# Rotary embedding: adding on VectorE alone, with one GpSimd product per tile

## The chip, the cores and the metric

The kernel runs on one core of a Trainium2 chip. The metric is device time in microseconds, the median of several executions. TensorE, VectorE (DVE in the profile), ScalarE (ACT), GpSimd (POOL) and SyncE (SP) run at the same time, each through its own queue of instructions, and wait for one another by semaphores. Transfers between the chip's memory (HBM) and the core's on-chip memory (SBUF, 128 partitions) are issued by SP and ACT and run on 16 DMA engines. PSUM is a second, small on-chip memory, which TensorE writes and which VectorE and ScalarE can read and write.

## What is computed

`x` has shape (8, 2048, 8, 64): batch, position, head, element. Each head's 64 elements are two halves of 32, which are rotated by an angle of their position:

```
x1, x2 = x[..., :32], x[..., 32:]
out1 = x1 * cos - x2 * sin
out2 = x1 * sin + x2 * cos
```

`cos` and `sin` have shape (2048, 32) and serve all batches and heads. All is float32. The input is 33.5 MB and the output as much.

## The kernel before

Each partition holds 16 consecutive positions ("rows") of one batch. A row is 8 heads of 64 elements, so 512 elements or 2 KB, and a batch is a tile `xt` of 128 partitions by 8192 elements, 32 KB in each partition and 4 MB in all. Five such buffers exist (`NBUF`). Batches 0 to 4 are loaded at the beginning from SP's queue, batch 0 in three parts (lines 64 to 71); batches 5 to 7 are loaded when the stores of batches 0 to 2 have left their buffers. Stores are issued from ACT's queue (line 74). All of these instructions are kept in program order on their queues.

A batch is worked in pieces of 4 rows (2048 elements); the first batch begins, and the last ends, with two pieces of 2 rows. `rotate` (line 101) knows three kinds of piece:

- Kind A, all pieces but the five named below: GpSimd makes `t2`, the other half times sine, in two instructions, one with `sin_sb` for the second halves and one with the negated table `nsin` for the first (line 121). VectorE makes `t1 = x * cos` in PSUM (line 128) and adds both back into `xt` (line 135).
- Kind B, the first piece of batches 2, 4 and 5: the products are the same, but TensorE adds them, by two matmuls with a unit matrix into PSUM (lines 140 and 141), and ScalarE copies the sum into `xt` (line 142).
- Kind C, the first piece of batches 1 and 3: VectorE makes both products (lines 128 and 145) and GpSimd none; TensorE adds or subtracts them with `eye` or `neye` (lines 156 and 157), and ScalarE copies (line 161).

`cos_ps` and `sin_ps` are copies of the tables in PSUM. The product `t2` has three buffers, so GpSimd can be ahead of VectorE by that many pieces; `t1` of kind A has one. The store of a whole batch is issued once its pieces are added; batch 0 is stored in parts of 1, 1, 2, 4 and 8 rows, each issued when the add that it depends on is done, and the last batch in parts of 8, 4 and 4 rows.

Of the kernel before, what the change touches and what calls it, by code (L numbers as in the profile page):

```python
# [9 lines left out]
@with_exitstack  # L10
def kernel(
    ctx: ExitStack,
    tc: tile.TileContext,
    x: bass.AP,
    cos: bass.AP,
    sin: bass.AP,
    out: bass.AP,
):
    nc = tc.nc
    keep = tc.keep_in_program_order  # L20
    f32 = mybir.dt.float32
    PSUM = bass.MemoryType.PSUM

    B, S, H, D = x.shape
    Dh = D // 2
    P = 128
    HD = H * D
    R = S // P
    ROW = R * HD
    UNIT = 4 * HD  # L30
    NBUF = 5
    C = 512
    last = B - 1

    xv = x.rearrange("b (q r) h d -> b q (r h d)", q=P)
    ov = out.rearrange("b (q r) h d -> b q (r h d)", q=P)
    cos_src = cos.rearrange("(q r) d -> q r d", q=P)
    sin_src = sin.rearrange("(q r) d -> q r d", q=P)

    const_pool = ctx.enter_context(tc.tile_pool(name="const", bufs=1))  # L40
    tab_pool = ctx.enter_context(tc.tile_pool(name="tab", bufs=1, space=PSUM))
    t1_pool = ctx.enter_context(tc.tile_pool(name="t1p", bufs=1, space=PSUM))
    o_pool = ctx.enter_context(tc.tile_pool(name="op", bufs=2, space=PSUM))
    t1s_pool = ctx.enter_context(tc.tile_pool(name="t1s", bufs=2))
    xpool = ctx.enter_context(tc.tile_pool(name="xpool", bufs=NBUF))
    t2_pool = ctx.enter_context(tc.tile_pool(name="t2p", bufs=3))

    cos_sb = const_pool.tile([P, R, Dh], f32, tag="cb")
    sin_sb = const_pool.tile([P, R, Dh], f32, tag="sb")
    nsin = const_pool.tile([P, R, Dh], f32, tag="ns")  # L50
    eye = const_pool.tile([P, P], f32, tag="eye")
    neye = const_pool.tile([P, P], f32, tag="neye")
    cos_ps = tab_pool.tile([P, R, Dh], f32, tag="cp")
    sin_ps = tab_pool.tile([P, R, Dh], f32, tag="sp")

    xts = {}

    def spans(sizes):
        lo = 0
        for n in sizes:  # L60
            yield lo, n
            lo += n

    def load(b):
        xt = xpool.tile([P, ROW], f32, tag="xt", name=f"xt{b}")
        for lo, n in spans([UNIT, UNIT, 2 * UNIT] if b == 0 else [ROW]):
            keep(nc.sync.dma_start(out=xt[:, lo : lo + n], in_=xv[b, :, lo : lo + n]))  # L67
            if b == 0 and lo == 0:
                keep(nc.sync.dma_start(out=cos_sb, in_=cos_src))  # L69
                keep(nc.sync.dma_start(out=sin_sb, in_=sin_src))  # L70
        xts[b] = xt

    def store(b, lo, n):
        keep(nc.scalar.dma_start(out=ov[b, :, lo : lo + n], in_=xts[b][:, lo : lo + n]))

    for b in range(NBUF):
        load(b)

    nc.gpsimd.memset(eye, 0.0)  # L79
    nc.gpsimd.affine_select(  # L80
        out=eye,
        in_=eye,
        compare_op=mybir.AluOpType.not_equal,
        fill=1.0,
        base=0,
        pattern=[[-1, P]],
        channel_multiplier=1,
    )
    keep(nc.scalar.mul(nsin, sin_sb, -1.0))  # L89
    keep(nc.scalar.copy(sin_ps, sin_sb))  # L90
    keep(nc.scalar.mul(neye, eye, -1.0))
    keep(nc.vector.tensor_copy(cos_ps, cos_sb))  # L92

    def rep(a, n):
        return dataclasses.replace(a, ap=[a.ap[0][:], a.ap[1][:], [0, n], a.ap[-1][:]])

    kinds = {}
    for b, kind in ((1, "C"), (2, "B"), (3, "C"), (4, "B"), (5, "B")):
        kinds[(b, 0)] = kind

    def rotate(b, lo, n):
        kind = kinds.get((b, lo), "A")
        xt = xts[b][:, lo : lo + n]
        r0 = lo // HD
        nr = n // HD
        xk = xt.rearrange("p (r k d) -> p r k d", r=nr, d=Dh)
        xu = xt.rearrange("p (g u d) -> p g u d", u=2, d=Dh)
        if kind == "A":
            t1 = t1_pool.tile([P, n], f32, tag="t1")
        else:  # L110
            t1 = t1s_pool.tile([P, n], f32, tag="t1s")
        if kind == "C":
            t2 = t1s_pool.tile([P, n], f32, tag="t1s")
        else:
            t2 = t2_pool.tile([P, n], f32, tag="t2")
        t1u = t1.rearrange("p (g u d) -> p g u d", u=2, d=Dh)
        t2u = t2.rearrange("p (g u d) -> p g u d", u=2, d=Dh)
        if kind != "C":
            for u, tab in ((1, sin_sb), (0, nsin)):
                keep(  # L120
                    nc.gpsimd.tensor_mul(  # L121
                        out=t2u[:, :, u, :].rearrange("p (r h) d -> p r h d", h=H),
                        in0=xu[:, :, 1 - u, :].rearrange("p (r h) d -> p r h d", h=H),
                        in1=rep(tab[:, r0 : r0 + nr, :], H),
                    )
                )
        keep(
            nc.vector.tensor_mul(  # L128
                out=t1.rearrange("p (r k d) -> p r k d", r=nr, d=Dh),
                in0=xk,  # L130
                in1=rep(cos_ps[:, r0 : r0 + nr, :], 2 * H),
            )
        )
        if kind == "A":
            keep(nc.vector.tensor_add(out=xt, in0=t1, in1=t2))  # L135
        elif kind == "B":
            for j in range(n // C):
                o = o_pool.tile([P, C], f32, tag="o")
                cs = slice(j * C, (j + 1) * C)
                nc.tensor.matmul(o, eye, t1[:, cs], start=True, stop=False)  # L140
                nc.tensor.matmul(o, eye, t2[:, cs], start=False, stop=True)  # L141
                keep(nc.scalar.copy(xt[:, cs], o))  # L142
        else:
            keep(
                nc.vector.tensor_mul(  # L145
                    out=t2.rearrange("p (r k d) -> p r k d", r=nr, d=Dh),
                    in0=xk,
                    in1=rep(sin_ps[:, r0 : r0 + nr, :], 2 * H),
                )
            )  # L150
            G = C // Dh
            for u in range(2):
                for j in range(n // 2 // C):
                    o = o_pool.tile([P, C], f32, tag="o")
                    gs = slice(j * G, (j + 1) * G)
                    nc.tensor.matmul(o, eye, t1u[:, gs, u, :], start=True, stop=False)  # L156
                    nc.tensor.matmul(  # L157
                        o, eye if u else neye, t2u[:, gs, 1 - u, :], start=False, stop=True
                    )
                    keep(  # L160
                        nc.scalar.copy(  # L161
                            xu[:, gs, u, :], o.rearrange("p (g d) -> p g d", d=Dh)
                        )
                    )

    def pieces(b):
        if b == 0:
            return [2 * HD, 2 * HD, UNIT, UNIT, UNIT]
        if b == last:
            return [UNIT, UNIT, UNIT, 2 * HD, 2 * HD]  # L170
        return [UNIT] * 4

    for b in range(B):
        done = 0
        outs = list(spans([2 * UNIT, UNIT, UNIT] if b == last else [ROW]))
        for lo, n in spans(pieces(b)):
            rotate(b, lo, n)
            done = lo + n
            while outs and sum(outs[0]) <= done:
                whole = outs.pop(0)  # L180
                if b == 0:
                    for part in spans([HD, HD, 2 * HD, UNIT, 2 * UNIT]):
                        store(b, *part)
                else:
                    store(b, *whole)
        if b + NBUF <= last:
            load(b + NBUF)

# [29 lines left out]
```

## Time and profile before

| | before |
|---|---|
| median of 10 executions | 163.63 us (163.4 to 164.75) |
| the profiled execution | 163.91 us, its span 162.1 us |
| VectorE busy | 140.1 us (86%) in 66 instructions |
| GpSimd busy | 138.9 us (86%) in 70 instructions |
| TensorE matmul busy | 47.2 us (29%) in 80 instructions |
| ScalarE busy | 14.3 us (9%) in 24 instructions |
| DMA | 67.65 MB, 417 GB/s over the span |

The span is the time between the first and the last event of the profiled execution; what lies between it and the execution's time is start and end outside the profile. Times in the profile's lines are microseconds from the span's start. Groups list the source line, the engine, the operation, what it writes and reads, the shape, the count, then total busy time, mean nanoseconds of one, and the idle time ahead of it with what ended that. Lines of DMA issues give the size and the median time from issue to landing.

### The profile page before, as it was taken

The numbers are of one execution on the slowest core, as the hardware profiler recorded it, in microseconds if no ns is written. First come the engines' busy times: TensorE is split into PE (matmuls) and PEld (weight loads), VectorE is DVE, ScalarE is ACT, GpSimd is POOL, SyncE is SP. The second block draws the span as 40 slices with busy tenths as digits, with TensorE's granted clock in tenths as the row PEclk, the third lists the DMA queues.
The fourth block names the chain that finished last, engine by engine and source line by source line (L and its number), as shares of the span: only waits on it lengthen the run. The fifth ranks groups of instructions, "written<-read, shape, count | busy, mean of one in ns | idle before, by whom it ended". The sixth has DMA issues, their size and how long they took to land.

```text
span 162.1 us, 470 instructions
## 1 busy us (share of the span) xinstructions
PE 47.2 (29%) x80; PEld 18.9 (12%) x80; DVE 140.1 (86%) x66; ACT 14.3 (9%) x24; POOL 138.9 (86%) x70
## 2 busy tenths in 40 slices
PE   0000000497009950892039903991000000000000
PEld 0000000142004410440023302340000000000000
DVE  0468999999999999999999999999999999999600
ACT  3300000013000220041001210121000000000000
POOL 1299999999999899999994999999999999996000
PEclk9999999999955795599655975599555555555555
DMA  5999999999999989998999999989999999999994
GB/s 186 418 439 493 437 420 412 412 420 437 437 469 396 412 376 433 477 429 388 469 420 404 493 390 420 485 388 429 471 412 412 469 412 420 461 412 416 429 412 174
DMA packets 3746, 67.65 MB, mean 417 GB/s; under 512 B 416, under 2 KB 416, under 8 KB 1056
## 3 DMA queue, kind: packets, MB, share of 16 engines
q1 hardware_dynamic: 1728, 34.08, 49.7%
q10 hardware_dynamic: 2016, 33.56, 48.2%
q14 instruction: 2, 0.02, 0.0%
HBM read 34.08 MB, written 33.55 MB: 417 GB/s over the span
## 4 chain that ended last, share of the span: by engine, by line
DVE 75%; POOL 9%; issue 6%; DMA 3%; SPq 0%; DVEq 0%; POOLq 0%
DVE t L128 40%; DVE xt L135 33%; POOL t L121 9%; DMA sin_sb<-in_sin_dram 3%; DVE t L145 3%; DVEq L135 0%; SPq L69 0%; SPq L67 0%; POOLq L121 0%
## 5 line engine op out<-in xcount | busy, mean ns | idle before, releaser
L121 POOL TENSOR_TENSOR t<-xt,sin_sb 128x1024 f32<-128x1024 f32 (+1 forms) x32 | 70.3, 2198 | 8.8 <-DMA sin_sb<-in_sin_dram 5.7
L128 DVE TENSOR_TENSOR t<-xt,cos_ps 128x2048 f32<-128x2048 f32 (+1 forms) x34 | 73.4, 2167 | 0.8
L121 POOL TENSOR_TENSOR t<-xt,nsin 128x1024 f32<-128x1024 f32 (+1 forms) x32 | 70.3, 2198 | 0.0
L135 DVE TENSOR_TENSOR xt<-t,t 128x2048 f32<-128x2048 f32 (+1 forms) x29 | 62.2, 2144 | 5.4 <-POOL t L121 2.5
L140 PE MATMUL o<-t,eye 128*128 128x512 f32 x24 | 17.9, 837 | 25.7 <-DVE t L128 25.7
L156 PE MATMUL o<-t,eye 128*128 128x512 f32 x16 | 10.7, 772 | 36.9 <-DVE t L128 36.9
L141 PE MATMUL o<-t,eye 128*128 128x512 f32 x24 | 15.4, 731 | 0.0
L142 ACT COPY xt<-o 128x512 f32<-128x512 f32 x12 | 7.0, 586 | 48.2 <-PE o L141 48.2
L140 PEld LDWEIGHTS o<-t,eye 128*128 128x128 f32 x24 | 5.8, 257 | 34.3 <-issue 34.3
L156 PEld LDWEIGHTS o<-t,eye 128*128 128x128 f32 x16 | 3.6, 248 | 41.6 <-POOL t L121 30.5
L161 ACT COPY xt<-o 128x512 f32<-128x512 f32 x8 | 4.7, 586 | 42.5 <-PE o L157 42.5
L141 PEld LDWEIGHTS o<-t,eye 128*128 128x128 f32 x24 | 6.2, 257 | 9.0 <-issue 9.0
L92 DVE COPY cos_ps<-cos_sb 128x512 f32<-128x512 f32 x1 | 0.7, 694 | 6.2 <-DMA cos_sb<-in_cos_dram 6.2
L157 PE MATMUL o<-t,neye 128*128 128x512 f32 x8 | 4.7, 694 | 0.2 <-DVE t L145 0.2
L145 DVE TENSOR_TENSOR t<-xt,sin_ps 128x2048 f32<-128x2048 f32 x2 | 4.6, 2280 | 0.0
L157 PE MATMUL o<-t,eye 128*128 128x512 f32 x8 | 4.1, 592 | 0.0
L157 PEld LDWEIGHTS o<-t,neye 128*128 128x128 f32 x8 | 1.8, 240 | 3.4 <-issue 3.4
L157 PEld LDWEIGHTS o<-t,eye 128*128 128x128 f32 x8 | 1.5, 190 | 1.9 <-issue 1.9
L89 ACT ACT_TABLE_LOAD x1 | 1.3, 1283 | 0.7 <-PEq L202 0.7
L89 ACT ACTIVATE nsin<-sin_sb 128x512 f32<-128x512 f32 x1 | 0.6, 630 | 4.9 <-DMA sin_sb<-in_sin_dram 4.9
L90 ACT COPY sin_ps<-sin_sb 128x512 f32<-128x512 f32 x1 | 0.6, 579 | 0.0
L79 POOL MEMSET eye<- 128x128 f32 x1 | 0.2, 205 | 0.3 <-POOLq L202 0.3
(6 smaller groups left out, 1.0 us busy)
## 6 DMA issues: line engine op xcount, KB each, us to landing
xt<-in_x_dram SPq DMA_DIRECT2D x7, 4096.0 KB, 28.1
out_dram<-xt ACTq DMA_DIRECT2D x6, 4096.0 KB, 33.4
out_dram<-xt ACTq DMA_DIRECT2D x2, 2048.0 KB, 24.3
out_dram<-xt ACTq DMA_DIRECT2D x3, 1024.0 KB, 11.4
xt<-in_x_dram SPq DMA_DIRECT2D x2, 1024.0 KB, 6.0
xt<-in_x_dram SPq DMA_DIRECT2D x1, 2048.0 KB, 11.4
out_dram<-xt ACTq DMA_DIRECT2D x2, 256.0 KB, 19.0
out_dram<-xt ACTq DMA_DIRECT2D x1, 512.0 KB, 32.7
```

The source lines that it names most:

```text
L89: keep(nc.scalar.mul(nsin, sin_sb, -1.0))
L92: keep(nc.vector.tensor_copy(cos_ps, cos_sb))
L121: nc.gpsimd.tensor_mul(out=t2u[:, :, u, :].rearrange("p (r h) d -> p r h d", h=H), in0=xu[:, :, 1 - u, :].rearrange("p (r h) d -> p r h d" ...
L128: nc.vector.tensor_mul(out=t1.rearrange("p (r k d) -> p r k d", r=nr, d=Dh), in0=xk, in1=rep(cos_ps[:, r0 : r0 + nr, :], 2 * H),)
L135: keep(nc.vector.tensor_add(out=xt, in0=t1, in1=t2))
L140: nc.tensor.matmul(o, eye, t1[:, cs], start=True, stop=False)
L141: nc.tensor.matmul(o, eye, t2[:, cs], start=False, stop=True)
L142: keep(nc.scalar.copy(xt[:, cs], o))
L145: nc.vector.tensor_mul(out=t2.rearrange("p (r k d) -> p r k d", r=nr, d=Dh), in0=xk, in1=rep(sin_ps[:, r0 : r0 + nr, :], 2 * H),)
L156: nc.tensor.matmul(o, eye, t1u[:, gs, u, :], start=True, stop=False)
L157: nc.tensor.matmul(o, eye if u else neye, t2u[:, gs, 1 - u, :], start=False, stop=True)
L161: nc.scalar.copy(xu[:, gs, u, :], o.rearrange("p (g d) -> p g d", d=Dh))
```

## The change

- All adds are made on VectorE; the unit matrices, the matmuls, ScalarE's copies and `sin_ps` are gone, and with them kinds B and C.
- Batches 1 to 7 are worked in three pieces of 6, 5 and 5 rows (3072, 2560 and 2560 elements). Batch 0 keeps its pieces of 2, 2, 4, 4 and 4 rows.
- GpSimd makes `t2` in one instruction per piece. A table `sgn` holds, for each row, minus sine and sine side by side. The instruction reads `xt` with the two halves of each head swapped, by a step of -32 elements between halves. ScalarE fills `sgn` in four passes, rows 0 to 3 first.
- Batch 0 is stored in parts of 1, 7 and 8 rows (2, 14 and 16 KB in a partition), the last batch in parts of 6, 5 and 5 rows. Each is issued as soon as its rows are added.

```diff
-    nsin = const_pool.tile([P, R, Dh], f32, tag="ns")
-    eye = const_pool.tile([P, P], f32, tag="eye")
-    neye = const_pool.tile([P, P], f32, tag="neye")
+    sgn = const_pool.tile([P, R, 2, Dh], f32, tag="sg")
     cos_ps = tab_pool.tile([P, R, Dh], f32, tag="cp")
-    sin_ps = tab_pool.tile([P, R, Dh], f32, tag="sp")
...
+    loads = {0: [4, 4, 8]}
+    pieces = {0: [2, 2, 4, 4, 4]}
+    stores = {0: [1, 7, 8], last: [6, 5, 5]}
...
-    keep(nc.scalar.mul(nsin, sin_sb, -1.0))
-    keep(nc.scalar.copy(sin_ps, sin_sb))
-    keep(nc.scalar.mul(neye, eye, -1.0))
+    for lo, hi in ((0, 4), (4, R)):
+        keep(nc.scalar.mul(sgn[:, lo:hi, 0, :], sin_sb[:, lo:hi, :], -1.0))
+        keep(nc.scalar.copy(sgn[:, lo:hi, 1, :], sin_sb[:, lo:hi, :]))
     keep(nc.vector.tensor_copy(cos_ps, cos_sb))
...
     def rotate(b, lo, n):
+        xt = xts[b][:, lo * HD : (lo + n) * HD]
+        t1 = t1_pool.tile([P, n * HD], f32, tag="t1")
+        t2 = t2_pool.tile([P, n * HD], f32, tag="t2")
+        swapped = dataclasses.replace(
+            xt,
+            offset=xt.offset + Dh,
+            ap=[part[:], [HD, n], [D, H], [-Dh, 2], [1, Dh]],
+        )
+        s = sgn[:, lo : lo + n, :, :]
+        signed = dataclasses.replace(
+            s, ap=[s.ap[0][:], [D, n], [0, H], [Dh, 2], [1, Dh]]
+        )
...
+        keep(
+            nc.gpsimd.tensor_mul(
+                out=t2.rearrange("p (r h u d) -> p r h u d", r=n, h=H, u=2),
+                in0=swapped,
+                in1=signed,
+            )
+        )
         keep(
             nc.vector.tensor_mul(
...
+        keep(nc.vector.tensor_add(out=xt, in0=t1, in1=t2))

     for b in range(B):
+        outs = list(spans(stores.get(b, [R])))
+        for lo, n in spans(pieces.get(b, [6, 5, 5])):
+            rotate(b, lo, n)
+            while outs and sum(outs[0]) <= lo + n:
+                so, sn = outs.pop(0)
+                cs = slice(so * HD, (so + sn) * HD)
+                keep(nc.scalar.dma_start(out=ov[b, :, cs], in_=xts[b][:, cs]))
         if b + NBUF <= last:
             load(b + NBUF)
```

More of the change, by code (lines that the diff above doesn't have):

```diff
@@ L29 @@
     ROW = R * HD
-    UNIT = 4 * HD
     NBUF = 5
-    C = 512
     last = B - 1
@@ L42 @@
     t1_pool = ctx.enter_context(tc.tile_pool(name="t1p", bufs=1, space=PSUM))
-    o_pool = ctx.enter_context(tc.tile_pool(name="op", bufs=2, space=PSUM))
-    t1s_pool = ctx.enter_context(tc.tile_pool(name="t1s", bufs=2))
     xpool = ctx.enter_context(tc.tile_pool(name="xpool", bufs=NBUF))
@@ L49 @@
     sin_sb = const_pool.tile([P, R, Dh], f32, tag="sb")
-    nsin = const_pool.tile([P, R, Dh], f32, tag="ns")
-    eye = const_pool.tile([P, P], f32, tag="eye")
-    neye = const_pool.tile([P, P], f32, tag="neye")
+    sgn = const_pool.tile([P, R, 2, Dh], f32, tag="sg")
     cos_ps = tab_pool.tile([P, R, Dh], f32, tag="cp")
-    sin_ps = tab_pool.tile([P, R, Dh], f32, tag="sp")
-    xts = {}
+    loads = {0: [4, 4, 8]}
+    pieces = {0: [2, 2, 4, 4, 4]}
+    stores = {0: [1, 7, 8], last: [6, 5, 5]}
     def spans(sizes):
@@ L62, in spans @@
             lo += n
+    xts = {}
     def load(b):
         xt = xpool.tile([P, ROW], f32, tag="xt", name=f"xt{b}")
-        for lo, n in spans([UNIT, UNIT, 2 * UNIT] if b == 0 else [ROW]):
-            keep(nc.sync.dma_start(out=xt[:, lo : lo + n], in_=xv[b, :, lo : lo + n]))
+        for lo, n in spans(loads.get(b, [R])):
+            cs = slice(lo * HD, (lo + n) * HD)
+            keep(nc.sync.dma_start(out=xt[:, cs], in_=xv[b, :, cs]))
             if b == 0 and lo == 0:
@@ L71, in load @@
         xts[b] = xt
-    def store(b, lo, n):
-        keep(nc.scalar.dma_start(out=ov[b, :, lo : lo + n], in_=xts[b][:, lo : lo + n]))
     for b in range(NBUF):
         load(b)
[L79 to L88, printed above, removed]
-    keep(nc.scalar.mul(nsin, sin_sb, -1.0))
-    keep(nc.scalar.copy(sin_ps, sin_sb))
@@ L91 @@
-    keep(nc.scalar.mul(neye, eye, -1.0))
-    keep(nc.vector.tensor_copy(cos_ps, cos_sb))
[L94 to L99, printed above, removed]
-    def rotate(b, lo, n):
[L102 to L126, printed above, removed]
@@ new lines @@
+    for lo, hi in ((0, 4), (4, R)):
+        keep(nc.scalar.mul(sgn[:, lo:hi, 0, :], sin_sb[:, lo:hi, :], -1.0))
+        keep(nc.scalar.copy(sgn[:, lo:hi, 1, :], sin_sb[:, lo:hi, :]))
+    keep(nc.vector.tensor_copy(cos_ps, cos_sb))
+    def rotate(b, lo, n):
+        xt = xts[b][:, lo * HD : (lo + n) * HD]
+        t1 = t1_pool.tile([P, n * HD], f32, tag="t1")
+        t2 = t2_pool.tile([P, n * HD], f32, tag="t2")
+        part = xt.ap[0]
+        swapped = dataclasses.replace(
[7 more added lines that the diff above has]
+        )
+        c = cos_ps[:, lo : lo + n, :]
+        cosines = dataclasses.replace(
+            c, ap=[c.ap[0][:], c.ap[1][:], [0, 2 * H], c.ap[-1][:]]
+        )
[5 more added lines that the diff above has]
+            )
+        )
@@ L127, in rotate @@
         keep(
             nc.vector.tensor_mul(
-                out=t1.rearrange("p (r k d) -> p r k d", r=nr, d=Dh),
-                in0=xk,
-                in1=rep(cos_ps[:, r0 : r0 + nr, :], 2 * H),
-            )
-        )
[L134 to L171, printed above, removed]
+                out=t1.rearrange("p (r k d) -> p r k d", r=n, d=Dh),
+                in0=xt.rearrange("p (r k d) -> p r k d", r=n, d=Dh),
+                in1=cosines,
+            )
+        )
+        keep(nc.vector.tensor_add(out=xt, in0=t1, in1=t2))
     for b in range(B):
-        done = 0
-        outs = list(spans([2 * UNIT, UNIT, UNIT] if b == last else [ROW]))
-        for lo, n in spans(pieces(b)):
+        outs = list(spans(stores.get(b, [R])))
@@ L177 @@
+        for lo, n in spans(pieces.get(b, [6, 5, 5])):
             rotate(b, lo, n)
[L178 to L185, printed above, removed]
+            while outs and sum(outs[0]) <= lo + n:
+                so, sn = outs.pop(0)
+                cs = slice(so * HD, (so + sn) * HD)
+                keep(nc.scalar.dma_start(out=ov[b, :, cs], in_=xts[b][:, cs]))
```

## Prediction, made before the changed kernel was run

> **What bounds the kernel now.** I read the page's slices first, to see whether one engine or the transfers set the pace. The first line is VectorE's busy tenths in 40 slices, then GpSimd's, the mean busy share of the 16 DMA engines, and the GB/s moved.
>
> ```profile
> DVE  0468999999999999999999999999999999999600
> POOL 1299999999999899999994999999999999996000
> DMA  5999999999999989998999999989999999999994
> GB/s 186 418 439 493 437 420 412 412 420 437 437 469 396 412 376 433 477 429 388 469 420 404 493 390 420 485 388 429 471 412 412 469 412 420 461 412 416 429 412 174
> ```
>
> Three things are full at once, and the DMA engines longest: VectorE stops at the 37th slice, the transfers run to the end. Next the windows of the whole span (columns: start:end, length, busy and instruction count of PE, PEld, DVE, ACT, POOL, then granted clock, DMA share, GB/s).
>
> ```profile
> 0.00:16.50 16.50, 0.00 (x0) 0.00 (x0) 7.90 (x7) 2.63 (x4) 10.21 (x13) 1.00 0.94 385
> 16.50:152.50 136.00, 47.22 (x80) 18.92 (x80) 132.16 (x60) 11.71 (x20) 128.72 (x58) 0.72 1.00 429
> 152.50:162.10 9.60, 0.00 (x0) 0.00 (x0) 0.04 (x1) 0.00 (x0) 0.00 (x0) 0.50 0.73 309
> ```
>
> In the middle stage the DMA share is 1.00 and VectorE is 97% busy. When VectorE ends, at 152.5, 9.6 us of transfers are still to come. So a store backlog ends this kernel, and VectorE has slack against it; how much decides the case. The transfers of 152 to 162.1 and their issue:
>
> ```profile
> DMA packets 373, 3.23 MB, mean 320 GB/s; under 512 B 48, under 2 KB 48, under 8 KB 48
> out_dram<-xt ACTq DMA_DIRECT2D x1, 1024.0 KB, 8.6
> ```
>
> The last store, 1024 KB, is issued at 152.6 and takes 8.6 us to land (161.2), because about 2.2 MB stand in front of it. At the 431 GB/s of the window from 128 to 152, which holds stores only, 1.05 MB alone take 2.4 us. The bare minimum for a last store on idle engines is taken from the first load: 1024 KB issued at 0.74, 4.7 us to landing. VectorE's slack is therefore about 8.6 - 4.7 = 3.9 us. More than that, and VectorE's end sets the time.
>
> Then the groups, shapes apart, for the prices:
>
> ```profile
> L128 DVE TENSOR_TENSOR t<-xt,cos_ps 128x2048 f32<-128x2048 f32 x30 | 68.5, 2292 | 0.7
> L121 POOL TENSOR_TENSOR t<-xt,nsin 128x1024 f32<-128x1024 f32 x28 | 65.4, 2334 | 0.0
> L135 DVE TENSOR_TENSOR xt<-t,t 128x2048 f32<-128x2048 f32 x25 | 57.3, 2292 | 3.8 <-POOL t L121 1.2 <-DVE t L128 0.4
> L121 POOL TENSOR_TENSOR t<-xt,nsin 128x512 f32<-128x512 f32 x4 | 5.0, 1247 | 0.0
> L128 DVE TENSOR_TENSOR t<-xt,cos_ps 128x1024 f32<-128x1024 f32 x4 | 4.9, 1229 | 0.1
> ```
>
> and the chain of waits at its start, to see who leads:
>
> ```profile
> 7.00 9.47 POOL t L121 x6
> 16.47 0.02 issue
> 16.49 2.30 DVE xt L135
> ```
>
> GpSimd leads up to 16.5; after it VectorE leads.
>
> **What the Trainium skill says.** "VectorE: DVE Perf Modes", section The TRN2 errata, gives (N+151)/0.96 ns for an fp32 tensor-tensor operation: 2291 at 2048, and the trace has 2292. "GPSIMD Engine Reference", section 3.1, gives 4497 ns for the same on GpSimd. The trace's halves, 1247 at 512 and 2334 at 1024, are a line of 160 ns plus 2.123 ns per element, 4508 at 2048: it agrees, although the halves read runs of 32. "SBUF — State Buffer", Who interferes with whom, says that a VectorE instruction with two SBUF inputs contends with GpSimd's reads. Each product and each add here has one input in PSUM (cos_ps or t1), before and after. "DMA: Bandwidth & Descriptors", Where 436 GB/s comes from, puts the ceiling at 435; the stores reach 431, so no packet size can bring much.
>
> **The change, part by part.**
>
> *Tile prices.* From the rows, an operation on VectorE takes 166 + 1.038 ns per element: 3.36 us at 3072 and 2.82 at 2560 (the skill's formula gives 3.36 and 2.82). A product and its add repeat every 4.72 us at 2048 (starts 88.20 and 92.92), which is 0.14 over 2 x 2.292. So a tile of 6 rows costs 6.86 and one of 5 rows 5.78: a batch costs 18.42 on VectorE. On GpSimd neighbouring instructions repeat every 2.28 us at 1024 and about 1.22 at 512, so overhead between them is slightly negative; one product takes 6.68 at 3072 and 5.60 at 2560, together 17.9, or about 17.7 at their repeat. GpSimd stays 4% quicker than VectorE.
>
> *Start.* GpSimd's first product waited for the sine load (6.85); now also for two quarter-size ScalarE passes into the signed table. The 128-column ScalarE row took 300 ns, so the first product begins near 7.4, not 7.0. Each tile then needs one instruction where it needed two, which saves about 0.15 a tile. Third tile: 7.4 + 2 x 2.28 + 4.50 = 16.5, as before. The other two passes, rows 4 to 15, are done by 8.3, before GpSimd's third product. Batch 0 ends at 28.2, as now. GpSimd's product for batch 1's first tile ends near 32.0 and VectorE's at 31.7, so that add waits 0.3 us.
>
> *TensorE part gone.* Batches 2, 4 and 5 gave away one add of four: they took 16.2, 16.2 and 16.5 us on VectorE (stores issued at 46.75, 63.01; 81.46, 97.70; then 114.16), and take 18.4: +2.2, +2.2, +1.9. Batches 1 and 3 gave GpSimd's product and the add away and did a second product instead: 18.5 each, now +0.3 (the wait above) and 0. Batch 6 was 19.0, now 18.4, and batch 7, with five tiles, 19.6, now 18.4: -0.6 and -1.2. Sum: +4.8. VectorE ends at 152.55 + 4.8 = 157.4. The 80 matmuls, 20 ScalarE copies and two PSUM buffers are off every path; their removal brings nothing by itself, and GpSimd gets two more tiles, within its 4%.
>
> *Stores of batch 0.* Parts of 1, 7 and 8 rows instead of 1, 1, 2, 4 and 8, issued behind the same adds except that rows 1 to 3 wait until 18.8. The stream is full of loads by then. Each part with longer rows takes a larger share beside 32 KB load rows, so buffer 0 comes free earlier and the sixth load leaves earlier than its present 63.4; the fifth load, which today leaves at 35.1 behind a small store, waits in the changed order for the third load of batch 0 instead and leaves near 14. Both reorder a stream that is at 1.00 anyway: nothing. If that cover failed, a batch would be late: the tightest of the three reloads today, batch 6, is issued at 79.1, lands 28.9 us later at 108.0 and is first used at 114.1, so 6 us are spare.
>
> *End.* The last store is 5 rows, 1.31 MB, issued at 157.4. All other bytes, 66.3 MB, would be through at 160.9 - 3.0 = 157.9 if the stream kept today's course, or up to 2 us sooner; so it meets a backlog of half a microsecond or none. Lower bound of its landing: 0.9 before the first byte (the first load: 0.74 to about 1.65), 3.04 for the bytes, 0.3 to land: 4.3. Upper bound: the first load's 4.7 plus 0.26 MB more, 5.3. I take 4.8. Landing at 157.5 + 4.8 = 162.3 and 0.9 from there to the end, as today (161.2 to 162.1): span 163.2, against 162.1, or +1.1. The profiled execution took 163.91, 1.81 around its span, and lies 0.28 above the median of 163.63. On the median: 164.8.
>
> **Rivals.**
> *VectorE ends last* (the above), 164.8, 164.1 to 165.7 with the two bounds and 0.3 us for the tile prices. For it: the 3.9 us slack is less than the 4.8.
> *Not slower: the backlog still ends last.* If VectorE ended by 156.6, or the last store landed in 4.1 us, the span would stay within 0.4 us of 162.1: 163.6 to 164.0. The point is 0.8 us away in a sum of 150 us; against it, every price is a measured row or a line through two. Earlier stores of batch 0 could also remove the small dips of the DMA line, which only helps while a backlog lasts.
> *Faster.* If the 21 larger tiles lost their 0.14 us of overhead, VectorE would end near 154.5; the last store then meets a backlog again, and if the larger first stores also smooth the slices below 9 of the DMA line, about 1.3 us, the span is 160.8: 162.3.
> *GpSimd becomes the bound.* Its product now walks pairs of 32-element runs backwards, a pattern no row shows. Below the line's price a gain moves only the first 32 us. Above it, the 4% reserve is used up first; at 5% the end moves by about 3 us (1.2 in the lead-in, then 0.15 a batch and the batch 1 tile): 167.5; at 10% by 9.5: 174. For the line's price: the skill's 4497 for a plain pattern equals what the halves give with runs of 32. I take the line.
> *The change doesn't do what it says* is excluded by its instruction order: one GpSimd product and two VectorE operations per tile, no matmul.
>
> **How the numbers follow.** About 0.3% (0.5 us) is what a measurement here can tell from no change. VectorE last 0.66, all of it slower; GpSimd the bound 0.13, slower; backlog last 0.15, the same; faster 0.06. Slower 0.79, same 0.15, faster 0.06. The range leaves out the faster case and GpSimd beyond 5%: 163.5 to 167.5; the likeliest case alone has 164.1 to 165.7.
>
> **What would show it.** Right: VectorE's last add near 157.4, three tiles a batch at 18.4; GpSimd idle before its products on VectorE's adds; the last store landing about 5 us after issue, not 8.6; a dip of the DMA line near 156 to 158. Wrong: GpSimd products over 6.9 us at 3072, VectorE adds idle on GpSimd in every batch, or a last store that lands 8 us after issue.

## The result and the profile after

| | before | after |
|---|---|---|
| median | 163.58 us (32 executions) | 164.91 us (9 executions) |
| ratio to before | | 1.0082, 95% interval 1.0068 to 1.0097 |
| profiled span | 162.1 us | 163.2 us |
| VectorE busy | 140.1 us in 66 instructions | 145.5 us in 53 |
| GpSimd busy | 138.9 us in 70 | 142.5 us in 30 |
| VectorE's last add ends | 152.5 | 157.8 |
| last store: issued, landed | 152.6, 161.2 | 157.9, 162.3 |

The change makes the kernel 0.8% slower, by 1.3 us. A second series of the changed kernel (the last experiment) gave 1.0050, interval 1.0028 to 1.0072, beside a kernel before that was 0.4 us slower there. In that series 8 of the 22 executions of the changed kernel took 167.6 to 170.7 us, and none of the kernel before more than 165.4; the ratios leave such long executions out, and the last two experiments come back to them.

The slices of the changed kernel's page: busy tenths of VectorE, GpSimd and the DMA engines, and GB/s.

```profile
DVE  0459899899999999999999999999999999999960
POOL 0199999999999999999999999999999999997000
DMA  5999998999999999999999999999999999998956
GB/s 181 416 440 495 435 412 366 415 474 412 398 458 474 410 394 490 402 410 474 402 474 426 386 482 418 396 466 410 442 450 402 466 426 402 426 458 364 436 221 281
```

VectorE now works into the last slice but one, where before it stopped in the last but two. The DMA line ends in 5 and 6, and the rate in 221 and 281: the stream, full before, has a hole. The windows show its place (columns: start:end, length, busy and count of VectorE, ScalarE, GpSimd, clock, DMA share, GB/s):

```profile
0.00:16.50 16.50, 7.90 (x6) 2.60 (x5) 9.15 (x7) 1.00 0.95 385
16.50:157.50 141.00, 137.30 (x47) 0.00 (x0) 133.34 (x24) 1.00 0.99 425
157.50:163.20 5.70, 0.34 (x1) 0.00 (x0) 0.00 (x0) 1.00 0.55 230
```

and closer, the transfers from 152 to the end, in 40 steps of 0.28 us:

```profile
DMA  3969939959995997810000009985992999400000
GB/s 132 702 263 439 571 132 600 402 219 549 549 402 219 585 475 329 366 37 37 0 0 0 0 37 549 585 366 219 585 549 110 512 585 402 183 0 0 0 0 0
```

From about 157.0 to 158.7 almost nothing moves: the earlier stores run out (the last of them lands at 157.8), and the final one is issued only at 157.9, behind VectorE's last add. What follows is that store alone.

The groups of the changed kernel, shapes apart:

```profile
L98 POOL TENSOR_TENSOR t<-xt,sgn 128x2560 f32<-128x2560 f32 x14 | 78.1, 5609 | 0.0
L98 POOL TENSOR_TENSOR t<-xt,sgn 128x3072 f32<-128x3072 f32 x7 | 46.8, 6691 | 0.0
L105 DVE TENSOR_TENSOR t<-xt,cos_ps 128x2560 f32<-128x2560 f32 x14 | 39.6, 2828 | 0.5
L105 DVE TENSOR_TENSOR t<-xt,cos_ps 128x3072 f32<-128x3072 f32 x7 | 23.5, 3361 | 0.2
L111 DVE TENSOR_TENSOR xt<-t,t 128x3072 f32<-128x3072 f32 x7 | 23.5, 3358 | 1.0 <-POOL t L98 0.4
```

The prices are those of the lines through the old sizes: 6.69 and 5.61 us against 6.68 and 5.60 for GpSimd, 3.36 and 2.83 against 3.36 and 2.82 for VectorE. Walking the halves in swapped order costs GpSimd nothing that shows. Its neighbouring products overlap by about 0.05 us: from start to start they take 6.64 and 5.55 us, so a batch takes GpSimd 17.75 us (seven batches from 25.57 to 149.84), 0.7 less than VectorE's 18.43. The chain of waits shows who leads, and from when:

```profile
24.79 0.78 issue
25.57 6.70 POOL t L98
32.26 0.02 issue
32.28 3.37 DVE xt L111
```

GpSimd leads up to the first add of batch 1, at 32.3, where the prediction had 32.0; from there on VectorE sets the pace to its end. The waits between the two (total, count, longest) agree:

```profile
POOL t L98 <- ACT sgn L76: 7.1, 1, 7.1
DVE xt L111 <- POOL t L98: 2.8, 3, 1.8
```

VectorE waits for GpSimd three times, the last time at 32.3. GpSimd waits only at its start, and never for VectorE: its last product ends at 149.8, 5.2 us before VectorE begins to add it.

### The profile page after: what moved, and what is told of

The parts are those of the page before. It is cut to its first block, busy times and chain, and to the rows that moved or that the text cites. A ratio compares the mean times of both kernels' runs of the same rounds, so it can differ in the third digit from the quotient of the medians.

```text
span 163.2 us, 217 instructions
## 1 busy us (share of the span) xinstructions
DVE 145.5 (89%) x53; ACT 2.6 (2%) x5; POOL 142.5 (87%) x30
## 4 chain that ended last, share of the span: by engine, by line
DVE 76%; POOL 13%; issue 4%; DMA 3%; SPq 0%; DVEq 0%; ACT 0%
DVE xt L111 39%; DVE t L105 37%; POOL t L98 13%; DMA sin_sb<-in_sin_dram 3%; DVEq L111 0%; SPq L67 0%; SPq L65 0%; ACT sgn L76 0%; ACT sgn L75 0%
## 5 line engine op out<-in xcount | busy, mean ns | idle before, releaser
L98 POOL TENSOR_TENSOR t<-xt,sgn 128x2560 f32<-128x2560 f32 (+3 forms) x26 | 142.3, 5524 | 7.1 <-ACT sgn L76 7.1
L111 DVE TENSOR_TENSOR xt<-t,t 128x2560 f32<-128x2560 f32 (+3 forms) x26 | 72.4, 2784 | 5.2 <-POOL t L98 2.8
L105 DVE TENSOR_TENSOR t<-xt,cos_ps 128x2560 f32<-128x2560 f32 (+3 forms) x26 | 72.5, 2787 | 0.9
L75 ACT ACTIVATE sgn<-sin_sb 128x128 f32<-128x128 f32 (+1 forms) x2 | 0.8, 413 | 5.0 <-DMA sin_sb<-in_sin_dram 5.0
L76 ACT COPY sgn<-sin_sb 128x128 f32<-128x128 f32 (+1 forms) x2 | 0.8, 387 | 0.0
```

Of the source, the lines that this page charges most:

```text
L75: keep(nc.scalar.mul(sgn[:, lo:hi, 0, :], sin_sb[:, lo:hi, :], -1.0))
L76: keep(nc.scalar.copy(sgn[:, lo:hi, 1, :], sin_sb[:, lo:hi, :]))
L98: nc.gpsimd.tensor_mul(out=t2.rearrange("p (r h u d) -> p r h u d", r=n, h=H, u=2), in0=swapped, in1=signed,)
L105: nc.vector.tensor_mul(out=t1.rearrange("p (r k d) -> p r k d", r=n, d=Dh), in0=xt.rearrange("p (r k d) -> p r k d", r=n, d=Dh), in1=cosines,)
```

## The experiments

The theory: VectorE's work puts its end past the stream's backlog, and the last store, alone, follows. The rivals: either the new parts of batch 0 cost the stream its rate, or GpSimd, whose product is new, sets the time. Times are compared with the kernel before on the same chip (163.75 to 164.02 there).

**TensorE's part taken out alone.** Kernel before, with

```diff
-    for b, kind in ((1, "C"), (2, "B"), (3, "C"), (4, "B"), (5, "B")):
+    for b, kind in ():
```

> The kernel before with every piece of kind A: TensorE's part alone is taken out; pieces of 4 rows and two GpSimd products stay. Theory: VectorE needs 18.9 us a batch and 19.6 for the last; from 28.2 on it ends at 161.1, 8.6 later than before; the last store of 1.05 MB is then exposed (4.2 to 4.7 us) and 0.9 follow: span 166.3 to 166.8, 167.6 to 168.3 us. Rival, the stream ends last in any case: 163.6 to 164.5.

Measured 168.02 us against 163.75, ratio 1.0252 (1.0212 to 1.0293). VectorE's last add ends at 161.35, 8.8 us later than before; the last store is issued right behind it and lands 3.9 us after its issue, as the theory has it. The part that the change removes was worth 4.3 us.

**One product instead of two.** Changed kernel, with

```diff
-    pieces = {0: [2, 2, 4, 4, 4]}
-    stores = {0: [1, 7, 8], last: [6, 5, 5]}
+    pieces = {0: [2, 2, 4, 4, 4], last: [4, 4, 4, 2, 2]}
+    stores = {0: [1, 7, 8], last: [8, 4, 4]}
...
-        for lo, n in spans(pieces.get(b, [6, 5, 5])):
+        for lo, n in spans(pieces.get(b, [4, 4, 4, 4])):
```

> The changed kernel with the pieces and last stores of before (4 rows; 4, 4, 4, 2, 2 in the last batch): this is the one without TensorE's part with one GpSimd product per piece in place of two, and the new parts of batch 0. Theory: VectorE leads, so one product or two makes no difference but the lead-in (0.2): 167.6 to 168.4, the same as the kernel without TensorE's part to 0.4 us; and the larger pieces of the change are worth the 3 us between this one and 164.9. Rival, the single product is what makes the changed kernel what it is (GpSimd bound): this one differs by 2 us or more from the other.

Measured 167.98, ratio 1.0243 (1.0203 to 1.0283): the same as the one above within 0.1 us. The groups and the repeats say why. GpSimd's two halves in the kernel without TensorE's part:

```profile
L121 POOL TENSOR_TENSOR t<-xt,nsin 128x1024 f32<-128x1024 f32 x30 | 71.1, 2371 | 0.0
L121 POOL TENSOR_TENSOR t<-xt,sin_sb 128x1024 f32<-128x1024 f32 x30 | 71.0, 2368 | 0.0
```

and GpSimd's single product in this one:

```profile
L98 POOL TENSOR_TENSOR t<-xt,sgn 128x2048 f32<-128x2048 f32 x30 | 134.3, 4509 | 0.4 <-DVE xt L111 0.4
```

These durations overlap by about 0.05 us at each neighbour, and by more towards the end of the run with two halves. From start to start the two halves take 4.56 us together and the single product 4.47, and both are less than the 4.72 that VectorE needs for its two operations. The difference between this kernel and the changed one, 3.1 us, is the worth of the larger pieces. VectorE's end goes from 161.4 to 157.8, 3.6 us sooner; eight pieces fewer, at the prediction's 2 x 0.166 us of fixed time and 0.14 of overhead each, would be 3.8. The last store, which is larger by 0.26 MB, takes 0.6 us of it back (4.5 us to landing, not 3.9).

**Batch 0 in the old parts.** Changed kernel, with

```diff
-    stores = {0: [1, 7, 8], last: [6, 5, 5]}
+    stores = {0: [1, 1, 2, 4, 8], last: [6, 5, 5]}
```

> The changed kernel with batch 0 stored in the parts of before (1, 1, 2, 4 and 8 rows). Theory: the parts reorder a stream that is full; 164.9, within 0.4 us either way. Rival, the new parts cost the stream its rate (its slices near 20 to 28 us show 366 to 418 GB/s): 163.9 to 164.4.

Measured 165.1, ratio 1.0089 (1.0055 to 1.0122), span 163.2 like the changed kernel's. The parts make no measurable difference to the time, although the sixth load leaves at 54.7 with the new ones and at 63.7 with the old. That speaks against the rival of a slower stream. The transfers of 20 to 30 us show why the load leaves earlier: packets, MB and share of the loads (q1) and the stores (q10), first with the old parts, then with the new.

```profile
q1 hardware_dynamic: 136, 3.93, 91.1%
q10 hardware_dynamic: 136, 0.25, 6.4%
q1 hardware_dynamic: 121, 3.44, 84.0%
q10 hardware_dynamic: 119, 0.75, 17.9%
```

Loads and stores start nearly the same number of packets, so the stores' share of the bytes grows with the length of their rows, as the prediction had it. It has a price that the time doesn't show: the load of the last batch lands at 131.2 with the new parts and at 128.2 with the old, and GpSimd begins on that batch at 132.0 in both. The changed kernel has 0.8 us to spare there, not 3.8.

**A shorter last store.** Changed kernel, with

```diff
-    pieces = {0: [2, 2, 4, 4, 4]}
-    stores = {0: [1, 7, 8], last: [6, 5, 5]}
+    pieces = {0: [2, 2, 4, 4, 4], last: [6, 5, 3, 2]}
+    stores = {0: [1, 7, 8], last: [6, 5, 3, 2]}
```

> The changed kernel with the last batch in pieces and stores of 6, 5, 3 and 2 rows, not 6, 5 and 5. Theory (VectorE's end plus the exposed last store): one piece more costs VectorE 0.47 us (3.66 + 2.60 in place of 5.79), its end goes from 157.8 to 158.3; the last store has 0.52 MB and not 1.31, which is 1.8 us less. Net -1.4: span 161.8, about 163.5 us. Rival, the stream is slower because of its new row lengths and ends last: 164.9 or more. Rival, GpSimd sets the end: 164.9 or a little more.

Measured 163.53 at the median of 11 executions, span 161.8, ratio 0.9985 (0.9966 to 1.0005); the other 11 took 166.1 to 170.9. This is the experiment that decides for the exposed store: VectorE ends 0.4 us later and the kernel 1.4 us sooner. The issues from 150 on (size and time to landing):

```profile
out_dram<-xt ACTq DMA_DIRECT2D x1, 1280.0 KB, 5.7
out_dram<-xt ACTq DMA_DIRECT2D x1, 768.0 KB, 3.8
out_dram<-xt ACTq DMA_DIRECT2D x1, 512.0 KB, 2.6
```

2.6 us for the last where the changed kernel has 4.5. At its best it brings the changed kernel level with the kernel before, not clearly ahead of it.

**More VectorE work in the changed kernel.** With the product of batch 3's first piece made twice:

```diff
+        if (b, lo) == (3, 0):
+            keep(
+                nc.vector.tensor_mul(
+                    out=t1.rearrange("p (r k d) -> p r k d", r=n, d=Dh),
+                    in0=xt.rearrange("p (r k d) -> p r k d", r=n, d=Dh),
+                    in1=cosines,
+                )
+            )
```

> The changed kernel with VectorE's product of batch 3's first piece made twice, 3.38 us more. Theory: all of it shows, 168.3. If the stream had slack over VectorE: less than 167.

Measured 168.54 (1.0314, 1.0247 to 1.0382); its profiled execution took 168.18 with a span of 166.4, 3.2 over the changed kernel's. Nearly all of the 3.38 us shows: VectorE has no slack there.

**More VectorE work in the kernel before.** The product of batch 6's second piece made two times (below), then four times (`range(3 ...)`):

```diff
+        for _ in range(1 if (b, r0) == (6, 4) else 0):
+            keep(
+                nc.vector.tensor_mul(
+                    out=t1.rearrange("p (r k d) -> p r k d", r=nr, d=Dh),
+                    in0=xk,
+                    in1=rep(cos_ps[:, r0 : r0 + nr, :], 2 * H),
+                )
+            )
```

> The kernel before with one VectorE product of batch 6 made twice, 2.3 us more on VectorE. Theory: inside the slack of 3.9 us, 163.6 to 163.9. If VectorE's end set the time of the kernel before: 165.9.

> The kernel before with one VectorE product of batch 6 made four times, 6.9 us more on VectorE. Theory: 3.9 us are hidden and 3.0 show: 166.6 (166.1 to 167.1). If the stream ended last in any case: 163.6; if VectorE's end set the time from the first: 170.5.

Measured 163.59 against 163.84 (ratio 0.9978, 0.9956 to 0.9999): 2.3 us more on VectorE cost nothing. With 6.9 us more, 166.13, 2.3 over (1.0145, 1.0093 to 1.0196). So 4.6 us of the 6.9 were hidden. In that run the last add is

```profile
158.23 1.23 DVE L143 TENSOR_TENSOR xt<-t,t 128x1024 f32<-128x1024 f32 x1
```

and its store, issued at 159.5, lands in 3.9 us. The prediction had taken the first load's 4.7 for a store without a backlog. With 3.9 its own sum gives 8.6 - 3.9 = 4.7, and by the spans (164.3 against 162.1, VectorE 6.9 later) 4.7 were hidden.

**Less VectorE work in the changed kernel.** Batch 3's first piece isn't added:

```diff
-        keep(nc.vector.tensor_add(out=xt, in0=t1, in1=t2))
+        if (b, lo) != (3, 0):
+            keep(nc.vector.tensor_add(out=xt, in0=t1, in1=t2))
```

> The changed kernel without the add of batch 3's first piece: that piece of the output is left as it was loaded. VectorE has 3.39 us less in its middle. Theory: VectorE ends at 154.4, and now the stream's backlog takes over, which without dry spells ends near 160.0: span 161.2, 162.9 us (162.3 to 163.3), a gain of 2.0 of the 3.4. If VectorE's end alone counted: 161.5. If the stream ended last already: 164.9.

Measured 163.59 (0.9981, 0.9962 to 1.0001), span 162.1: 1.3 us less at the median and 1.1 in the span, where 2.0 were expected. The timeline behind the missing add shows what went otherwise (the first line is two products in a row):

```profile
65.73 6.22 DVE L105 TENSOR_TENSOR t<-xt,cos_ps 128x3072 f32<-128x3072 f32 x2
73.47 2.83 DVE L112 TENSOR_TENSOR xt<-t,t 128x2560 f32<-128x2560 f32 x1 [1.52 <-POOL t L98]
```

VectorE arrives early and waits 1.52 us for GpSimd's product. In the changed kernel that product is done at 73.30 and its add begins at 75.49, so GpSimd is only 2.2 us ahead there, and VectorE can't gain 3.4. The last store is issued at 156.3, 1.55 us sooner and not 3.4, and takes 4.9 us to land, 0.4 more than in the changed kernel. GpSimd's lead was left out of the expectation.

**More GpSimd work in the changed kernel.** One row more in each piece of 6 rows:

```diff
+        if n == 6:
+            keep(
+                nc.gpsimd.tensor_mul(
+                    out=t2[:, :HD].rearrange("p (r h u d) -> p r h u d", r=1, h=H, u=2),
+                    in0=dataclasses.replace(swapped, ap=[part[:], [HD, 1], *swapped.ap[2:]]),
+                    in1=dataclasses.replace(signed, ap=[s.ap[0][:], [D, 1], *signed.ap[2:]]),
+                )
+            )
```

> The changed kernel with the GpSimd product of one row (512 elements) made a second time in the first piece of batches 1 to 7, about 1.21 us more of GpSimd a batch, 6.8%. Theory: GpSimd has 0.57 us a batch to spare (17.85 against 18.43), so it becomes the bound: GpSimd ends at 25.6 + 7 x 19.06 = 159.0 and the last add follows, VectorE's end 161.85, +4.0: 168.9. Rival, GpSimd is far from the bound and the addition is hidden: 164.9 to 165.5. If GpSimd had been the bound already: +8.5, 173.4.

Measured 170.41 (1.0397, 1.0365 to 1.0429), 5.5 us over the changed kernel and 1.5 over the expectation. The waits, with total, count and longest:

```profile
DVE xt L119 <- POOL t L106: 6.3, 7, 1.8
```

One wait in each of the seven batches: GpSimd is the bound here. GpSimd's last product ends at 159.2, as expected (159.0). The miss is in what follows: VectorE waits at the piece of 6 rows, where the extra row is, and then has its own two pieces of 5 rows to do, 11.6 us, which it does more slowly than GpSimd; its end is 163.05 and not 161.85.

**The first sine product on VectorE.** Changed kernel, with (`sgn_ps` is a PSUM copy of the table's first two rows)

```diff
...
+        if (b, lo) == (0, 0):
+            sp = sgn_ps[:, 0:2, :, :]
+            second = nc.vector
+            signed = dataclasses.replace(
+                sp, ap=[sp.ap[0][:], [D, n], [0, H], [Dh, 2], [1, Dh]]
+            )
+        else:
+            second = nc.gpsimd
         keep(
-            nc.gpsimd.tensor_mul(
+            second.tensor_mul(
...
```

> The changed kernel with the sine product of the very first piece (2 rows) made on VectorE, from a copy of the signed table in PSUM, so that GpSimd begins with the second piece. VectorE idles 2.8 us on GpSimd in the lead-in and gets 1.3 us of work for it. Theory: VectorE ends 1.4 us sooner, 156.4, and so does the kernel: 163.5 (163.2 to 163.9). Rival, the stream ends last: 164.9.

and the same with the last batch in 6, 5, 3 and 2 rows:

> Both: the first sine product on VectorE and the last batch in 6, 5, 3 and 2 rows. Theory: VectorE ends at 156.9, and the stream's own end near 160.0 is met: span 161.0 to 161.4, 162.7 to 163.2 us, less than the sum of both gains (162.1) and below the 163.6 of the kernel before.

Neither met its expectation: six executions of each gave medians of 170.49 and 169.37, and the best took 166.81 and 166.35. Two things are visible. First, the gain on VectorE is 0.55 us and not 1.4: batch 6 begins at 120.47 where the changed kernel has 121.02. The sine product stands ahead of the cosine product in VectorE's queue and waits until 7.86 for the table, while the cosine product could have run. The second of the two kernels has about the same gain: VectorE ends at 157.6, where the shorter last store alone has 158.2. Second, loads come late. The chain of the first of the two:

```profile
97.67 41.50 DMA xt<-in_x_dram
139.17 0.02 issue
139.20 0.02 POOLq L109
139.21 0.09 issue
139.31 6.68 POOL t L109
```

The load of batch 7 takes 41.5 us. The changed kernel has 37.5 for it (93.7 to 131.2). In the trace 14 of its 16 completions stand between 129.5 and 130.8, two at 138.9 and 139.2. "DMA: Bandwidth & Descriptors" of the Trainium skill, section Why a DMA increments its semaphore by 16, says that the semaphore counts the engines and that only the full 16 means that all has landed; so GpSimd waits for the slowest, and the trace agrees: its product begins at 139.31. In the trace of the second kernel, six of the 16 completions of this load come 3 to 5 us behind the first ten. That the quicker start shortens the kernel is therefore not shown, and not excluded.

**The changed kernel again,** without an edit.

> The changed kernel once more, unaltered, in many executions beside the kernel before. It asks whether the two DMA engines that fell 9.7 us behind in the run with the first sine product on VectorE belong to that edit or to the changed kernel as well. If it is the edit: 164.9 in nearly all executions. If the changed kernel has it too, as often as the one with the finer tail (12 of 22 executions over 1.5% above its fastest): half of the executions between 166 and 171.

Measured 164.84 at the median of 14 executions, and 167.6 to 170.7 in the other 8. (With the shorter last store it was 11 of 22, not 12.) The long executions thus belong to the changed kernel as well; they are no effect of that edit alone. That late engines make them long here too is likely but not shown: the profiled execution is one of the 14, with all 16 completions of batch 7's load within 1.2 us and a span of 162.9.

What sets the delay off isn't settled. One pattern stands out: with batch 0 stored in 1, 7 and 8 rows, 30 of the 99 executions of the changed kernel and its variants were over 1.5% above the fastest of their kernel; with 1, 1, 2, 4 and 8 rows, in the changed kernel and in the variants of the kernel before, none of 36 was. The spare time of 0.8 us for the last load, where the old parts leave 3.8, would fit. But only 7 of the 36 differ from the changed kernel in the parts alone, too few to tell.

## Why the prediction was right

Predicted 164.8, measured 164.91; span predicted 163.2, measured 163.2. By its steps:

- *Tile prices.* Right to 0.01 us. A batch takes 18.43 on VectorE (18.42), and 17.75 on GpSimd from start to start, close to the 17.7 of the prediction; the reserve is just under 4%. About 7% more work on GpSimd costs 5.5 us, so the rival in which GpSimd becomes the bound was close by. It didn't come true because the swapped pattern costs nothing. (The contention that the prediction cites isn't tested: no VectorE product or add of any run here has both inputs in SBUF.)
- *Start.* First product at 7.55 (7.4), batch 1's first add at 32.28 (32.0). The single product saves 0.09 us a tile from start to start (4.56 to 4.47), not the 0.15 that the prediction read from the durations. Batch 0 ends 0.25 us later than predicted, and VectorE waits 0.45 us and not 0.3 at batch 1: these two are the whole error of VectorE's end.
- *TensorE's part gone, larger pieces.* The sum was +4.8, to 157.4; measured 157.84, +5.3. The two experiments split it: removing TensorE's part moves VectorE's end by +8.8, the larger pieces by -3.6.
- *Stores of batch 0 at nothing.* Right for the time: 165.1 with the old parts. They did reorder the loads as said (the fifth load leaves at 14.35, the sixth at 54.65). The spare time of the reloads was misread: the prediction counted to VectorE's first use of batch 6, but GpSimd reads it from 111.48 on, 3.5 us after its landing and not 6, and batch 7 is tighter (landed at 127.3, read from 129.75). In the changed kernel 0.8 us are left.
- *End.* The last store was taken at 4.8 and needs 4.5; it met no backlog but a dry stream. This makes up for most of the 0.4 that VectorE's end is later. That the two errors cancel is luck, and so is the agreement to 0.1 us; the mechanism is shown by the shorter last store. With measured terms the sum is: VectorE 5.3 us later, 4.7 of it hidden, and 0.6 more for the larger last store, 1.2; the span grew by 1.1.
- *The slack of the kernel before.* Predicted 3.9, measured 4.6 to 4.7. The term that was mis-sized is the time of a bare last store, taken from a load of the same size, 4.7, where the store needs 3.9. It enters only the point from which the rival of no change decides, and moves it by 0.7 to 0.8 us towards that rival; the sum for the change itself used a value between the bounds.
- *Rivals.* No backlog ended the changed kernel, so the case of no change didn't come. Nor did the faster case: the 0.14 us of overhead stayed (a piece of 6 rows repeats after 6.86 us, for two operations of 3.36), and the stream wasn't smoothed (425 GB/s from 16.5 to 157.5, against 429 in the middle stage before).
- *Signs.* VectorE's end, the 18.4 us of a batch, the short landing of the last store and the dip of the DMA line came as named. One sign did not: GpSimd never waited for VectorE. It gains 0.7 us a batch from no lead at batch 1 on, so its lead reaches 5.2 us only at the end, and the three `t2` buffers never hold it up. (VectorE's last busy slice before is the 38th, not the 37th.)

## What to carry to other kernels

When three resources are all near 90%, read off each one's reserve in microseconds from the end of the kernel: here 4.7 for VectorE against the stream's backlog, and 0.7 a batch for GpSimd against VectorE, which has to build up before it can be used. In these kernels, work moved to an engine was free up to that reserve and counted nearly in full beyond it. Count the spare time of a load to the first engine that reads it. Where an engine's end sets the time, the last transfer is as good as serial with it, so cut the last piece small: here 0.79 MB less in the last store was worth 1.4 us net of the extra instructions.

## What was not expected of the hardware

- A store of 1.05 MB that meets an idle stream lands 3.9 us after its issue, one of 1.31 MB after 4.5 and one of 0.52 MB, behind the end of an earlier store, after 2.6; the first load of 1.05 MB needed 4.7. Why the load takes longer wasn't tested.
- While loads and stores share the engines they start nearly equal numbers of packets, although the sizes differ: 136 and 136 from 20 to 30 us with the old parts of batch 0, for 3.93 and 0.25 MB.
- GpSimd reads pairs of 32-element runs in swapped order at the price of plain ones: 4509 ns at 2048 elements, where "GPSIMD Engine Reference" of the Trainium skill, section 3.1, gives 4497 for the plain operation.
- Two of the 16 DMA engines can end a 4 MB load 8 to 9 us after the other 14 (129.5 to 130.8, then 138.9 and 139.2); what sets it off stays open.
